# First FFN's up projection: transposing gated tiles into the other factor's buffer, and one adding transfer of each quad as an add on VectorE

## The chip, the cores and the metric

The kernel runs on one core of a Trainium2 chip. Its engines work side by side, each through its own instructions in order: TensorE (PE in the profile; PEld is its loading of weights), VectorE (DVE), ScalarE (ACT), GpSimd (POOL) and SyncE (SP, which here only issues transfers). Sixteen DMA engines carry the transfers; those of SyncE go out on the hardware queue q1, those of GpSimd on the software queue q0. The metric is the device time of one execution in microseconds.

## The reference

One layer of a diffusion backbone on 256 context and 256 latent tokens of width 2048: a half-step FFN, a mixer (attention heads beside bidirectional mLSTM heads), a second half-step FFN on the latent tokens, and a final norm, all with conditioned norms. The change touches only the first half-step FFN, which runs on all 512 tokens:

```python
def half_step_ffn(x, mod, i, g, w_up, w_down):
    h = adaln(x, g, mod, i)
    a, b = jnp.split(h @ w_up, 2, axis=-1)
    return x + 0.5 * mod[:, i + 2, None, :] * ((jax.nn.silu(a) * b) @ w_down)
```

The width of the hidden layer is 5632, that is 11 blocks of 512 columns. `mod` comes from the conditions through a weight matrix of its own (`w_mt` here), all of it in float32.

## The kernel before

**Products.** Every float32 product is made as three products of a rounded part and a rest (`hi` and `lo`): `hi*hi`, `hi*lo`, `lo*hi` (`mm3`, L152). So each weight tile of 128 x 2048 is split before use, in two halves of 1024 columns: ScalarE writes `hi` (L128), VectorE subtracts and writes `lo` (L129). There are four buffers of each, two tiles' worth. Where a helper records operations, the profile gives the helper's line for all of its callers.

**Up projection, block 0** is made beside the opening of the kernel. **Blocks 1 to 10** are made one after the other by `quad(n)`. It is a scheme of seven products instead of eight on halves of the token block and of the depth: the left factors are the token forms `a11, a12, n1, s4, s2, s3, a22` (fixed, made once, held in SBUF), the right ones are sums of weight parts, and the results add up in PSUM banks `X`, `Y`, `Z`. The list `order` has the seven with their sources; each is done for `q` = 0 and 1, one weight tile each, so that a quad has 14 steps, numbered 0 to 13 here (step 2m + q), of 24 products each.

**Where the weight sums come from.** `part(n, ab, c)` is a stored tile of 1 MB: ab = 0 for the gate's weights A, 1 for the other factor's B. Two tiles `chain_[q]` stay for the stage. At steps 0 and 1 they hold an A part. As soon as a step has split its tile, GpSimd issues an adding transfer (`accum`, L740) that adds the next part into it: a B part for `n1` (steps 4 and 5), another B part for `s2` (steps 8 and 9), another A part for `a22` (steps 12 and 13); then `again` loads the next quad's first part. Steps 2 and 3 use tiles loaded plain (`plain`, L910). Steps 6 and 7 use `ra[q]`, loaded by `loaded` (L905), the same B part that was added to `chain_[q]` after step 4 or 5; then a further part is added into `ra[q]`, which serves steps 10 and 11. That makes eight adding transfers in a quad. The tiles of `plain` and `loaded` are the four users of three buffers (`raw_tile`), in turn.

**The way out of PSUM.** At the end of a product, `use` copies or adds banks on ScalarE and VectorE: `p1` and `c11` make one gate tile in `ca` (silu on ScalarE, L868 and L890), `kept` copies a bank to `cy`, `p35` one to `c12`; `c12`, `c22` and `c21` add the second bank and multiply gate and other factor into `ca` (L851, L852). `ca`, `cy` and `c12` have two buffers each. A finished `ca` tile is put on the list `turn`. At the next step with q = 0, after half of its products, `turned` takes one from it: VectorE transposes it in blocks into the one buffer `stg` (L842) and SyncE stores `stg` to the hidden tensor in HBM (L844). The tiles of a quad are so stored at its steps 10 and 12 and at steps 0 and 2 of the next.

**Beside it** run the products of the modulation (`mod_items`): 96 weight tiles of 512 KB through two `sraw` buffers, issued by SyncE (L237), each multiplied and summed by VectorE (L208) with condition vectors of the context and the latent tokens in `cBh`. The vectors cover half of the depth; at half way both are loaded anew (L203), and the code holds the products back three steps (`WAIT = 3`).

**Down projection.** It begins with `pair(0)`: VectorE makes sums of hidden tiles by `first_plan`, and results go to `acc` (first copies L1078, adds L1080), in memory that the up stage's tiles had.

**The order of the work.** Each engine's order is fixed when the kernel is built, by a planner that takes instructions as their inputs and buffers come free by its costs, and otherwise as the code has them; instructions given to `keep_in_program_order` (`pinned`) keep their order among each other. Waits for data and for buffers are then added.

Of the kernel before, what the change touches and what calls it, by code (L numbers as in the profile page):

```python
# [9 lines left out]
F32 = mybir.dt.float32  # L10
# [9 lines left out]
P = 128  # L20
# [15 lines left out]
N_HID = 3  # L36

N_TURN = 2

PACE = (4, 2), (12, 13), (19, 19), (27, 28), (35, 37), (42, 44), (51, 51), (58, 54), (65, 61), (70, 70), (73, 76), (74, 85), (79, 96)  # L40
PACE += (86, 102), (92, 109), (98, 118), (100, 130), (103, 144), (106, 152), (109, 163), (112, 170), (128, 181)
# [5 lines left out]
CB = 512  # L47
# [11 lines left out]
def tile_layer(ctx: ExitStack, tc: tile.TileContext, I: dict, out: bass.AP):  # L59
    nc = tc.nc  # L60
# [12 lines left out]
    def bank():  # L73
        return ps["mm"].tile([P, 512], F32, tag="mm", name="mm")
# [619 lines left out]
    hidd = [dr.tile([4, P, CB] if n else [P, 16, P], F32, name=f"hid{n}") for n in range(NF // FB)]  # L694
# [6 lines left out]
    def form(tag, name):  # L701
        sp = ft if tag == "t" else fm
        return [sp.tile([P, 2, 8, P], F32R, tag=f"{tag}{x}", name=f"{name}{x}") for x in "hl"]
# [9 lines left out]
    def pinned(ins):  # L713
        tc.keep_in_program_order(ins)
# [22 lines left out]
    chp = chcm.__enter__()  # L737

    chain_ = [chp.tile([P, 2048], F32, name=f"chain{c}") for c in range(2)]
    accum = lambda dst, src: nc.gpsimd.dma_start(dst, src, accum_op=ALU.add)  # L740
    with pool(name="f1u", bufs=1) as f1u:
# [7 lines left out]
        def ca_tile():  # L749
            return f1u.tile([P, CB], F32, tag="ca", name="ca", bufs=2)  # L750
# [9 lines left out]
        def part(n, ab, c):  # L760
            return I["w_up1b"][n - 1, ab, c]

        def first_chain(n, c):
            nc.sync.dma_start(chain_[c], part(n, 0, c))
# [16 lines left out]
        n1, s2, s4 = form("n", "n1"), form("s", "s2"), form("t", "s4")  # L781
# [3 lines left out]
        a11, a12, a21, a22 = quarter(0, 0), quarter(0, 1), quarter(1, 0), quarter(1, 1)  # L785
# [43 lines left out]
        forms = token_forms()  # L829
        steps(forms, 2)  # L830
        turn = []
        last_turn = []

        def turned():

            if not turn:
                return
            n, t, ca = turn.pop(0)

            def staged():  # L840
                stg = chp.tile([P, CB], F32, tag="stg", name="stg")
                pinned(nc.vector.transpose(stg, ca))  # L842
                s, tt = divmod(t, 2)
                nc.sync.dma_start(hidd[n][2 * tt + s], stg)  # L844

            if (n, t) == (NB - 1, 3):
                last_turn.append(staged)
            else:
                staged()

        add = lambda o, x, y: nc.vector.tensor_tensor(o, x, y, op=ALU.add)  # L851
        negative = lambda o, y: nc.vector.scalar_tensor_tensor(o, o, -1.0, y, op0=ALU.mult, op1=ALU.mult)  # L852

        def c12_tile():
            return f1u.tile([P, CB], F32, tag="c12", name="c12", bufs=2)

        def quad(n, after=lambda step: None):

            X, Y, Z = {}, {}, {}
            ca, cy, cb, ra = {}, {}, {}, {}  # L860

            def p1(s):
                ca[s] = ca_tile()
                nc.scalar.activation(ca[s], X[s], AF.Copy)

            def c11(s):
                add(ca[s], Z[s], ca[s])
                nc.scalar.activation(ca[s], ca[s], AF.Silu)  # L868

            def kept(s):  # L870
                cy[s] = f1u.tile([P, CB], F32, tag="cy", name="cy", bufs=2)
                nc.scalar.activation(cy[s], Y[s], AF.Copy)

            def p35(s):
                cb[s] = c12_tile()
                nc.scalar.activation(cb[s], Y[s], AF.Copy)

            def c12(s):
                add(cb[s], X[s], cb[s])
                negative(ca[s], cb[s])  # L880
                turn.append((n, 2 * s, ca[s]))

            def c22(s):
                add(cy[s], X[s], cy[s])
                ca[s] = ca_tile()
                nc.scalar.activation(ca[s], X[s], AF.Copy)

            def c21(s):
                add(ca[s], Y[s], ca[s])
                nc.scalar.activation(ca[s], ca[s], AF.Silu)  # L890
                negative(ca[s], cy[s])
                turn.append((n, 2 * s + 1, ca[s]))

            def chained(ab, c):
                return lambda q: accum(chain_[q], part(n, ab, c + q))

            def again(q):
                if n + 1 < NB:
                    first_chain(n + 1, q)
                else:  # L900
                    nc.sync.dma_start(chain_[q], I["w_dn1"][0, 2 * q])

            def loaded(q):
                ra[q] = raw_tile()
                nc.sync.dma_start(ra[q], part(n, 1, 2 + q))  # L905
                return ra[q]

            def plain(q):
                r = raw_tile()
                nc.sync.dma_start(r, part(n, 0, 2 + q))  # L910
                return r

            held = lambda q: chain_[q]
            order = (
                (a11, held, X, True, chained(1, 0), p1),
                (a12, plain, Z, True, None, c11),
                (n1, held, Y, True, chained(1, 2), kept),
                (s4, loaded, Y, False, lambda q: accum(ra[q], part(n, 1, q)), p35),
                (s2, held, X, False, chained(0, 2), c12),
                (s3, lambda q: ra[q], X, False, None, c22),  # L920
                (a22, held, Y, True, again, c21),
            )
            for m, (a, src, dst, fresh, then, use) in enumerate(order):
                if fresh:
                    dst.update({s: bank() for s in range(2)})
                for q in range(2):
                    wt = split(src(q))
                    if then:
                        then(q)
                    after(2 * m + q)  # L930
                    for s in range(2):
                        for j in range(4):
                            k = 4 * q + j
                            hi, lo = a[0][:, s, k, :], a[1][:, s, k, :]
                            mm3(dst[s], hi, lo, *wt(slice(j * CB, (j + 1) * CB)), fresh and k == 0, k == 7, True)
                        if q and use:
                            use(s)
                        elif not s:
                            turned()
# [123 lines left out]
    def pair(p):  # L1063

        X, Y, Z, ra = {}, {}, {}, {}
# [8 lines left out]
        w = lambda m, cb: I["w_dn1"][2 * p + m, cb]  # L1074
# [41 lines left out]
        def loaded(m, cb):  # L1116
            raw = raw_tile()
            nc.sync.dma_start(raw, w(m, cb))
            return raw
# [9 lines left out]
        held = lambda c: chain_[c]  # L1129
# [14 lines left out]
        for m, (g, src, dst, fresh, then, use) in enumerate(order):  # L1144
            a = place0[m] if p == 0 and m < 2 else place[g]
            for c in range(2):
                wt = split(src(c))
                if then:
                    then(c)
                added()  # L1150
                if p == 0 and 2 * m + c == 1:
                    last_turn.pop()()
                for x in todo.get(2 * m + c, "").split():
                    if x.startswith("raw"):
                        hid_load(2 * p + 2 + int(x[3]), raws[int(x[3])])
                    else:
                        make[x]()
                if p == NP - 1:
                    if (2 * m + c) in GATES:
                        ahead.append(both_gates(GATES[2 * m + c]))  # L1160
                    if 2 * m + c == 13:
                        last_gate(0)
                        last_gate(1)
                    if m in (1, 4, 6):
                        gates = used[c] = ahead.pop(0)
                    elif m == 5:
                        gates = used[c]
                for s in range(2):
                    if fresh:
                        dst[c, s] = tbank() if c and dst is not X else bank()  # L1170
                    for j in range(FB):
                        k = slice((2 * j + s) * P, (2 * j + s + 1) * P)
                        mm3(dst[c, s], a[:, 0, k], a[:, 1, k], *wt(slice(j * CB, (j + 1) * CB)), fresh and j == 0, j == FB - 1, True)
                    use(c, s)
# [92 lines left out]
    with ExitStack() as mx:  # L1267
# [626 lines left out]
        for cb in range(NCB):  # L1894
# [8 lines left out]
            c = slice(cb * CB, (cb + 1) * CB)  # L1903
# [36 lines left out]
    with f2x:  # L1940
# [66 lines left out]
        a11, a12, a21, a22 = quarter(0, 0), quarter(0, 1), quarter(1, 0), quarter(1, 1)  # L2007
        forms2 = {g: f3.tile([P, 2, 8, P], F32R, tag=f"f{i}", name=f"{g}f") for i, g in enumerate(("n1", "s4", "s2", "s3"))}
        n1, s4, s2, s3 = ([x[:, 0], x[:, 1]] for x in (forms2[g] for g in ("n1", "s4", "s2", "s3")))
# [39 lines left out]
        turn = []  # L2049
        summed = set()  # L2050
        born, clock = {}, [0]

        def turned():
# [3 lines left out]
            n, t, sa, sign = turn[0]  # L2057
            if clock[0] < born[n, t] + N_TURN:
                return
# [383 lines left out]
```

## Time and profile before

| | us |
|---|---|
| runs | 2604.68, 2603.30, 2600.16 |
| median | 2603.3 |
| the profiled execution, its time | 2598.59 |
| its span | 2596.9 |
| TensorE busy | 2559.5 |
| VectorE busy | 2205.3 |
| ScalarE busy | 1404.3 |
| quads 1 to 10 | about 156 to 934 |
| mean granted TensorE clock | 0.993 of full |

Lines of the profile read so: start, duration, engine, line, operation, out<-in, shapes, count; in brackets the idle time of the engine just before it and what ended it. A group's line has total and mean duration, then the idle time before its members. The DMA lines give count, size and the median time from issue to landing. Matmuls overlap in the pipeline: each is shown with 0.39 us, and they start 0.227 us apart when nothing stops them.

### The profile page before, as it was taken

The page shows a single profiled execution, that of the slowest core. Times are in us where ns is not written, and L with a number is a line of the kernel's source. Part 1 is how long each engine was busy: PE and PEld are TensorE (multiplying, and loading weights), DVE is VectorE, ACT ScalarE, POOL GpSimd, SP SyncE. Part 2 cuts the span into 40 slices and gives each one's busy share as a digit, 9 for nine tenths or more (in the row PEclk, how much of TensorE's full clock was granted, in tenths as well). Part 3 has the DMA queues.
Part 4 walks back from the last instruction along what each step waited for, and adds up shares of the span by engine and source line. Part 5 has one row for each costly group of instructions (what it writes and reads, how often), then busy time and mean ns, then how long its engine had stood idle before and what let it go on. Part 6 is the DMA issues. An engine that isn't in the chain of part 4 may idle for free. (4 is left out here: it accounts for less than half of the span.)

```text
span 2596.9 us, 33840 instructions
## 1 busy us (share of the span) xinstructions
PE 2559.5 (99%) x12486; PEld 2126.6 (82%) x12486; DVE 2205.3 (85%) x2924; ACT 1404.3 (54%) x1798; POOL 222.0 (9%) x271
## 2 busy tenths in 40 slices
PE   8999999999999999999999999999999999999998
PEld 5788888878887878888889989888898888888886
DVE  7789888878888788888887899798889888888987
ACT  4454444444444455444454448456476676666763
POOL 0000000100000100000110000120000000000001
PEclk8999999999999999999999999999999999999999
DMA  9889999999999989999986897776768999999985
GB/s 395 348 217 276 267 284 277 263 269 279 264 290 269 263 239 243 212 221 233 225 256 256 292 328 241 241 277 218 266 230 248 275 272 279 285 282 279 272 250 167
DMA packets 153477, 684.69 MB, mean 264 GB/s; under 512 B 22872, under 2 KB 43864, under 8 KB 92000
## 3 DMA queue, kind: packets, MB, share of 16 engines
q1 hardware_dynamic: 123936, 490.64, 51.5%
q0 software_dynamic: 29376, 191.90, 37.2%
q8 instruction: 98, 1.61, 0.2%
q14 instruction: 67, 0.55, 0.1%
HBM read 664.59 MB, written 17.89 MB: 263 GB/s over the span
## 5 line engine op out<-in xcount | busy, mean ns | idle before, releaser
L128 ACT ACTIVATE hi<-raw 128x1024 fp32r<-128x1024 f32 (+2 forms) x488 | 504.3, 1040 | 401.7 <-PE mm L152 304.1
L129 DVE TENSOR_TENSOR lo<-raw,hi 128x1024 fp32r<-128x1024 f32 (+2 forms) x476 | 566.4, 1202 | 109.6 <-ACT hi L128 91.4
L128 ACT ACTIVATE hi<-chain 128x1024 fp32r<-128x1024 f32 x352 | 369.9, 1059 | 351.6 <-PE mm L152 200.4
L129 DVE TENSOR_TENSOR lo<-chain,hi 128x1024 fp32r<-128x1024 f32 x352 | 424.4, 1218 | 88.8 <-ACT hi L128 78.9
L152 PE MATMUL mm<-lo,hhi 128*128 128x512 f32 (+3 forms) x1024 | 388.3, 379 | 6.4 <-DVE lo L129 6.3
L152 PE MATMUL mm<-hi,hhi 128*128 128x512 f32 (+3 forms) x1024 | 390.9, 382 | 0.0
L152 PE MATMUL mm<-hi,hlo 128*128 128x512 f32 (+3 forms) x1024 | 387.1, 378 | 0.0
L208 DVE SCALAR_TENSOR_TENSOR junk<-sraw,cBh 128x1024 fp8e5<-128x1024 f32 x192 | 234.1, 1219 | 38.1 <-DMA sraw<-in_w_mt 36.3
L152 PEld LDWEIGHTS mm<-lo,hhi 128*128 128x128 f32 x1024 | 193.1, 189 | 42.2 <-DVE lo L129 8.7
L152 PEld LDWEIGHTS mm<-hi,hlo 128*128 128x128 f32 x1024 | 193.3, 189 | 32.2
L152 PEld LDWEIGHTS mm<-hi,hhi 128*128 128x128 f32 x1024 | 193.3, 189 | 31.8
L129 DVE TENSOR_TENSOR lo<-ra,hi 128x1024 fp32r<-128x1024 f32 x104 | 126.0, 1221 | 25.7 <-ACT hi L128 22.0
L128 ACT ACTIVATE hi<-ra 128x1024 fp32r<-128x1024 f32 x104 | 110.0, 1061 | 65.7 <-PE mm L152 39.7
L152 PE MATMUL mm<-lo,hid2h 128*128 128x512 f32 x352 | 137.1, 390 | 0.1
L152 PE MATMUL mm<-hi,hid2h 128*128 128x512 f32 x352 | 137.0, 389 | 0.0
L152 PE MATMUL mm<-hi,hid2l 128*128 128x512 f32 x352 | 137.0, 389 | 0.0
L152 PE MATMUL mm<-hi,sumshl 128*128 128x512 f32 x400 | 123.2, 389 | 0.0
L740 POOL DMA_DIRECT2D chain<-in_w_up1b x60 | 53.1, 886 | 734.2 <-DVE lo L129 573.8
L208 DVE SCALAR_TENSOR_TENSOR sr<-sr,cBl 128x1024 f32<-128x1024 f32 x84 | 102.1, 1223 | 14.0 <-DMA sr<-in_w_mt 13.1
L152 PE MATMUL mm<-hi,sumshh 128*128 128x512 f32 x352 | 108.9, 391 | 1.3 <-DVE acc L1080 1.3
L152 PE MATMUL mm<-hhi,hi 128*128 128x512 f32 (+1 forms) x288 | 101.4, 352 | 0.0
L152 PE MATMUL mm<-hhi,lo 128*128 128x512 f32 (+1 forms) x288 | 99.0, 344 | 0.0
(488 smaller groups left out, 5416.2 us busy)
## 6 DMA issues: line engine op xcount, KB each, us to landing
raw<-in_w_dn SPq DMA_DIRECT2D x70, 1024.0 KB, 9.8
chain<-in_w_up1b POOLq DMA_DIRECT2D x60, 1024.0 KB, 10.7
sraw<-in_w_mt SPq DMA_DIRECT2D x96, 512.0 KB, 8.5
sr<-in_w_mt SPq DMA_DIRECT2D x81, 512.0 KB, 5.5
raw<-in_w_up1b SPq DMA_DIRECT2D x40, 1024.0 KB, 9.1
mraw<-in_w_m SPq DMA_DIRECT2D x32, 1024.0 KB, 7.5
chain<-in_w_dn POOLq DMA_DIRECT2D x30, 1024.0 KB, 10.0
chain<-in_w_up2b POOLq DMA_DIRECT2D x28, 1024.0 KB, 10.5
```

The source lines that it names most:

```text
L128: scalar[0].activation(hi, src, AF.Copy)
L129: vector[0].tensor_tensor(lo, src, hi.bitcast(F32), op=ALU.subtract)
L152: tensor[0].matmul(out_ap, s, m, start=first and not n, stop=last and n == 2, skip_group_check=skip)
L208: ins = nc.vector.scalar_tensor_tensor(junk() if junk else raw, raw, 1.0, cB[s], op0=ALU.mult, op1=ALU.mult, accum_out=mT[:, i, s, kt, h : ...
L740: accum = lambda dst, src: nc.gpsimd.dma_start(dst, src, accum_op=ALU.add)
```

## The change

Two parts. First, each entry of `turn` carries along the tile of the other factor (`cb[s]`, of the pool's tag `c12`, or `cy[s]`), and the transpose writes into that tile instead of `stg`. Only the very last tile of the stage, whose store may outlast the pool, still goes to `stg`; it is transposed with the others at the end of the up stage, where before it was put off to step 1 of `pair(0)`.

Second, in quads 2 to 10, for q = 0 alone, the B part that was added to `chain_[0]` by a transfer after step 4 is added by VectorE from `ra[0]`, which holds the same part: half of it in step 5, the other half in step 6. `ra[0]` is for that asked for in step 3 instead of step 6. The transfer that then adds a further part into `ra[0]` comes behind the second add. For q = 1 everything stays.

```diff
+SUMMED = (0,)
...
-            n, t, ca = turn.pop(0)
-
-            def staged():
-                stg = chp.tile([P, CB], F32, tag="stg", name="stg")
-                pinned(nc.vector.transpose(stg, ca))
-                s, tt = divmod(t, 2)
-                nc.sync.dma_start(hidd[n][2 * tt + s], stg)
-
+            n, t, ca, spare = turn.pop(0)
             if (n, t) == (NB - 1, 3):
-                last_turn.append(staged)
-            else:
-                staged()
+                spare = chp.tile([P, CB], F32, tag="stg", name="stg")
+            pinned(nc.vector.transpose(spare, ca))
+            s, tt = divmod(t, 2)
+            nc.sync.dma_start(hidd[n][2 * tt + s], spare)
...
-                turn.append((n, 2 * s, ca[s]))
+                turn.append((n, 2 * s, ca[s], cb[s]))
...
-                turn.append((n, 2 * s + 1, ca[s]))
+                turn.append((n, 2 * s + 1, ca[s], cy[s]))
...
+            own = SUMMED if n > 1 else ()
+
+            def summed(q, h):
+                w = slice(h * 1024, (h + 1) * 1024)
+                add(chain_[q][:, w], chain_[q][:, w], ra[q][:, w])
+
+            def second(q):
+                if q not in own:
+                    chained(1, 2)(q)
+                if q - 1 in own:
+                    summed(q - 1, 0)
+
+            def third(q):
+                if q in own:
+                    if q == 1:
+                        summed(q, 0)
+                    summed(q, 1)
+                accum(ra[q], part(n, 1, q))
+
             held = lambda q: chain_[q]
             order = (
                 (a11, held, X, True, chained(1, 0), p1),
-                (a12, plain, Z, True, None, c11),
-                (n1, held, Y, True, chained(1, 2), kept),
-                (s4, loaded, Y, False, lambda q: accum(ra[q], part(n, 1, q)), p35),
+                (a12, plain, Z, True, lambda q: q - 1 in own and loaded(q - 1), c11),
+                (n1, held, Y, True, second, kept),
+                (s4, lambda q: ra[q] if q in own else loaded(q), Y, False, third, p35),
...
-                if p == 0 and 2 * m + c == 1:
-                    last_turn.pop()()
```

More of the change, by code (lines that the diff above doesn't have):

```diff
@@ L831, in tile_layer @@
         turn = []
-        last_turn = []
         def turned():
```

## The prediction

> **What bounds the kernel now.** I read the page's busy times first, then what TensorE waited for in the stage that the change touches, then that stage cut into its quads, and last the lines around the stalls.
>
> ```profile
> PE 2559.5 (99%) x12486; PEld 2126.6 (82%) x12486; DVE 2205.3 (85%) x2924; ACT 1404.3 (54%) x1798; POOL 222.0 (9%) x271
> ```
>
> ```profile
> PE mm L152 <- DVE lo L129: 9.1, 5, 3.5
> ```
>
> The second line is the whole list of TensorE's waits from 140 to 930 us: five, all for a `lo` half that VectorE had not yet written. Now the same stage, one window for each quad, from its first product with `n1` (step 4 of 14) to the next quad's:
>
> ```profile
> core 0: us, PE busy (x) PEld busy (x) DVE busy (x) ACT busy (x) POOL busy (x), PEclk, DMA share, GB/s
> 177.55:253.71 76.16, 76.16 (x338) 63.06 (x336) 62.00 (x77) 36.05 (x41) 7.07 (x8) 1.00 0.98 263
> ...
> 406.05:483.86 77.81, 76.94 (x337) 62.84 (x336) 68.36 (x90) 35.32 (x40) 7.09 (x8) 1.00 0.97 273
> 483.86:567.42 83.56, 79.54 (x337) 64.95 (x336) 64.36 (x83) 35.92 (x41) 7.95 (x9) 0.96 0.97 272
> 567.42:643.58 76.16, 76.16 (x338) 63.08 (x336) 65.53 (x84) 35.59 (x40) 6.26 (x8) 1.00 0.98 269
> 643.58:719.99 76.41, 76.41 (x339) 63.11 (x338) 67.58 (x94) 35.66 (x40) 6.98 (x8) 1.00 0.98 271
> ...
> 796.19:877.32 81.13, 78.19 (x338) 63.97 (x336) 70.31 (x92) 37.19 (x42) 7.94 (x9) 0.98 0.99 278
> ```
>
> Every window holds the same matmuls, about 337. An unstalled one takes 76.16 us with TensorE busy throughout, so the stage cannot go below that. Above it lie 1.65 (77.81), 7.40 (83.56), 0.25 (76.41) and 4.97 us (81.13): 14.3 us in all. That is what the change can win in these quads. VectorE works 62 to 70 us of each window and the DMA engines are busy 0.97 to 0.99 of it, so both are nearly full behind TensorE.
>
> **The transposes, the large stall.** Queries of VectorE, SyncE and TensorE around 545 us, with the landing of the store issued at 545.02:
>
> ```profile
> 557.65 0.71 DVE L842 STREAM_TRANSPOSE stg<-ca 128x512 f32<-128x512 f32 x1 [8.69 <-DMA hid<-stg]
> 558.29 2.31 DVE L129 TENSOR_TENSOR lo<-raw,hi 128x1024 fp32r<-128x1024 f32 x2
> ...
> 540.32 0.33 SPq L203 DMA_DIRECT2D cBh<-ccd  x1
> ...
> 542.44 0.49 SPq L203 DMA_DIRECT2D cBh<-ccd  x1
> 545.02 0.33 SPq L844 DMA_DIRECT2D hid<-stg  x1
> ...
> 559.52 0.80 PE L152 MATMUL mm<-lo,hhi 128*128 128x512 f32 x1 [3.54 <-DVE lo L129]
> ...
> DMA to landing us min/median/max: 12.5/12.5/12.5
> ```
>
> There is one `stg`. The second transpose of a pair may not overwrite it before the first one's store has landed. Here that store stands behind two 512 KB loads of the condition vectors and takes 12.5 us; VectorE, which works in order, waits 8.69 us with the next `lo` halves queued behind the transpose, and TensorE runs dry. The idle 3.54 us is followed by a granted clock of 0.96 over the window; idle and slow clock together are the 7.40 us.
>
> After the change each transpose writes the tile of its own other factor (`c12` or `cy`, two each), which VectorE itself has just finished reading. The wait has no cause left: **-7.40 us**. What is late next there? The `hi` halves for these products were done at once after (the `lo` needed no wait at 558.29), and the store may now take its time until its tile is taken again. For `cy` that is step 5 of the next quad, for `c12` step 7. The second `cy` transpose belongs to step 2, so three steps are left, 3 x 76.16/14 = 16.3 us, against a longest landing of 12.5 us. Behind a `cy` tile not yet free would stand ScalarE's copy `kept` of a PSUM bank, and behind that the products of step 6, which add into the same bank. The cover is thin by 3.8 us at the worst landing seen, ample at the median. I cost it at nothing.
>
> The transposes themselves stay, 702 ns each, and no DMA is added or dropped by this part. The very last one, of quad 10, moves from step 1 of the first down pair to the end of the stage, ahead of that pair's sums of hidden tiles on VectorE. Before:
>
> ```profile
> 938.94 0.70 DVE L842 STREAM_TRANSPOSE stg<-ca 128x512 f32<-128x512 f32 x1
> ...
> 943.72 0.71 DVE L842 STREAM_TRANSPOSE stg<-ca 128x512 f32<-128x512 f32 x1 [1.83 <-DMA hid<-stg]
> ...
> 944.52 1.58 ACT L1078 ACTIVATE acc<-mm 128x512 f32<-128x512 f32 x3 [4.32 <-issue]
> ...
> DMA to landing us min/median/max: 2.3/6.4/12.5
> ```
>
> (The last line is that of all 40 stores.) It no longer waits 1.83 us. But the first copies into `acc` start right when the last reader of the up stage's tiles ends (944.43), as their memory is the same; now a store reads from that memory too. Issued at about 939.7, it lands at 946.1 by the median, 1.7 us later than 944.43. So between -1.8 and, with 12.5 us, +7.8 us; I take **0**, the middle of no wait and a median store.
>
> **The add moved to VectorE.** Rows of the groups and of the DMA queues over 253 to 878 us, and of the same kind of add as the second FFN has it:
>
> ```profile
> L208 DVE SCALAR_TENSOR_TENSOR junk<-sraw,cBh 128x1024 fp8e5<-128x1024 f32 x169 | 206.1, 1219 | 37.9 <-DMA sraw<-in_w_mt 36.3
> ...
> L842 DVE STREAM_TRANSPOSE stg<-ca 128x512 f32<-128x512 f32 x32 | 22.5, 702 | 14.2 <-DMA hid<-stg 14.2
> ...
> q0 software_dynamic: 9238, 67.29, 54.6%
> ...
> chain<-in_w_up1b POOLq DMA_DIRECT2D x48, 1024.0 KB, 10.7
> ...
> raw<-in_w_up1b POOLq DMA_DIRECT2D x16, 1024.0 KB, 13.3
> ...
> L2089 DVE TENSOR_TENSOR chain<-chain,ra x20: 1212/1216/1226, 1978.6 to 2484.2; 128x1024 f32<-128x1024 f32 x20
> ```
>
> *Removed*: nine transfers, one in each of quads 2 to 10, each 0.88 us of issue on GpSimd, which is nearly idle. The 48 + 16 adding transfers hold all engines for 0.546 x 624 us / 64 = 5.3 us each. The factor was loaded twice (once added, once as `ra`), so this traffic goes away altogether. *Added*: 18 adds of 1.216 us on VectorE, 2.43 us a quad, and no load: `ra[0]` is asked for three steps earlier in the code, but the third staging buffer decides when it goes out. *Waits*: the first add of a quad needs `ra[0]`, and the transfer into `ra[0]` now waits for the second one. `ra[0]` is an old load by then: in the quad of 308 us its transfer went out at 290.78, some 45 us before step 5.
>
> ```profile
> 290.78 0.33 SPq L905 DMA_DIRECT2D raw<-in_w_up1b  x1
> ```
>
> Behind the adds on VectorE stand the `lo` halves of steps 6 and 7. Where these have no room the adds stall TensorE:
>
> ```profile
> 338.23 2.35 DVE L129 TENSOR_TENSOR lo<-raw,hi 128x1024 fp32r<-128x1024 f32 x2
> ...
> 344.42 2.35 DVE L129 TENSOR_TENSOR lo<-raw,hi 128x1024 fp32r<-128x1024 f32 x2
> ...
> 341.23 0.39 PE L152 MATMUL mm<-lo,s4h 128*128 128x512 f32 x1
> ...
> 346.67 0.39 PE L152 MATMUL mm<-lo,s4h 128*128 128x512 f32 x1
> ...
> 415.37 4.63 DVE L129 TENSOR_TENSOR lo<-raw,hi 128x1024 fp32r<-128x1024 f32 x4
> ...
> 417.41 0.39 PE L152 MATMUL mm<-lo,s4h 128*128 128x512 f32 x1
> ```
>
> In the quad of 308 us the first half for step 6 was ready at 339.4 and used at 341.23 (room 1.8), for step 7 at 345.6 and used at 346.67 (room 1.1): the one add ahead of step 6 fits, the two ahead of step 7 are 2.43 - 1.1 = 1.3 too long. In the quad of 384 us step 6 has 0.9 of room (416.5 to 417.41): 0.3 too long. In the others I take VectorE's present waits, 36.3 us for the `sraw` loads and 14.2 us for `stg`, as the room: together more than the 21.9 us of adds. **+1.7 us**, rounded up from 1.6; the bounds are nothing and all 18 adds, 21.9 us.
>
> **The relief of the DMA.** The other stall, in the window of 81.13:
>
> ```profile
> 810.21 2.35 DVE L129 TENSOR_TENSOR lo<-raw,hi 128x1024 fp32r<-128x1024 f32 x2
> 818.10 1.23 DVE L208 SCALAR_TENSOR_TENSOR junk<-sraw,cBh 128x1024 fp8e5<-128x1024 f32 x1 [5.54 <-DMA sraw<-in_w_mt]
> ...
> 805.64 0.33 SPq L237 DMA_DIRECT2D sraw<-in_w_mt  x1
> ...
> DMA to landing us min/median/max: 12.4/12.4/12.4
> ...
> 798.40 0.88 POOL L740 DMA_DIRECT2D chain<-in_w_up1b  x1 [15.64 <-DVE lo L129]
> ...
> 808.29 0.88 POOL L740 DMA_DIRECT2D raw<-in_w_up1b  x1 [3.79 <-DVE lo L129]
> ...
> 821.80 0.80 PE L152 MATMUL mm<-lo,s2h 128*128 128x512 f32 x1 [2.82 <-DVE lo L129]
> ```
>
> VectorE waits 5.54 us for a modulation load that took 12.4 us while adding transfers were in flight. The one issued at 798.40 is the one that goes. By its median landing of 10.7 it was in flight until 809.1, 3.5 us of the load's time. TensorE stood only 2.82 us, so a load 3.5 us shorter would have spared it all; but the adds put the load's issue up to 1.2 us later. Between 0 and -4.97 us; I take half, **-2.5 us**.
>
> Against this stands the Trainium skill, "DMA: Bandwidth & Descriptors", section "Queues, rings and completion order": each DMA engine alternates between the queues that have work, a packet at a time. By it the load's share does not depend on how many adding transfers are queued, only on whether one is. This trace has others in flight beside the load in any case, which agrees, and no run here yet shows the load without one; by it this term is 0.
>
> **The sum.** -7.4 + 0 + 1.7 - 2.5 = -8.2 us on the profiled execution's 2598.59: 2590.4. That execution is 4.7 us below the median of the runs shown (2603.3), so on that scale 2595.1. The quads' smaller excesses I leave as they are.
>
> **Rivals.**
> (1) *All stalls of these quads go*, since VectorE's waits for DMA shrink everywhere: -14.3, 2589.0. For it: each stall ends on a `lo` that VectorE brought late after such a wait. Against: VectorE gets 2.43 us more in the same quads.
> (2) *VectorE becomes the bound at steps 5 to 7* and shows its adds to TensorE: 18 x 1.216 - 7.4 = +14.5, 2617.8. For it: rooms of 1.1 and 0.9 us. Against: the unstalled windows with VectorE busy at 62 to 68 of 76 us. It decides from (7.4 + 5.2)/1.216 = 10 shown adds on, with 5.2 us (0.2%) as about what a measurement here can tell from no change.
> (3) *The stall at 545 us keeps its length with another owner*: the condition vectors issued at 542.44 are awaited by the next modulation product, which also stands in VectorE's queue. If it is ordered ahead of the `lo` halves VectorE waits nearly as long; 7.4 stays, 2.5 goes and 1.7 comes: -0.8, 2602.5. Against: the code holds these products back three steps after that load.
> (4) *The modulation loads gain nothing*, as other adding transfers are in flight beside them: -7.4 + 1.7 = -5.7, 2597.6. For it: another, issued at 808.29, ran beside the load of 12.4 us. By the page's rule just named, this is the case to expect.
>
> **How the numbers follow.** Forecast 0.38, (1) 0.20, (2) 0.13, (3) 0.14, (4) 0.15. The range runs from 2585 (rival 1, and the end of the stage at its best) to 2606 (rival 2 with half its adds shown: 10.9 - 7.4 = +3.5, 2606.8). Faster by over 0.2%: 0.36 of the forecast's, all of (1), 0.09 of (4), 0.65 in all; slower: (2) and 0.02 for a late store at the stage's end, 0.15; the rest, 0.20, is within.
>
> **What would show it.** Right: no wait of a transpose for a store, the window around 545 us at 76.2, the row of adds at 18 x 1.22, adding transfers from `w_up1b` 71 instead of 80, and the window around 820 us between 76 and 79. Wrong: TensorE waiting for `lo` at steps 6 and 7 in several quads (rival 2), ScalarE's copy into `cy` waiting for a store, or a new wait for `sraw` or the condition vectors where the large stall was.

## The result and the profile after

| | before | after |
|---|---|---|
| median, 8 runs each, same comparison | 2601.53 us | 2593.14 us |
| lowest and highest | 2596.10, 2604.68 | 2590.05, 2594.61 |
| ratio, 95% interval | | 0.9968 (0.9959 to 0.9978) |
| the profiled execution | 2598.59 | 2593.71 |

The kernel became 8.4 us faster, by the medians. The forecast was 8.2 us. (In a later comparison its ratio was 0.9981, 0.9972 to 0.9989, that is 5.1 us by the medians; the two intervals overlap.) The total is right, but two of its four terms were much too small, and they have opposite signs.

The busy times of the changed kernel come first, then all that TensorE waited for from 130 to 930 us:

```profile
PE 2557.9 (99%) x12486; PEld 2123.5 (82%) x12486; DVE 2223.8 (86%) x2942; ACT 1403.2 (54%) x1798; POOL 213.8 (8%) x262
```

```profile
PE mm L154 <- DVE lo L131: 3.9, 5, 2.4
```

VectorE has its 18 instructions more (2942 against 2924) and GpSimd its nine fewer. TensorE's waits fell from 9.1 to 3.9 us, and all are still for a `lo` half. The same windows as before, from the first product with `n1` of one quad to the next quad's (start:end, length, busy time of each engine, granted clock, DMA share, GB/s; the last row is all nine quads together):

```profile
core 0: us, PE busy (x) PEld busy (x) DVE busy (x) ACT busy (x) POOL busy (x), PEclk, DMA share, GB/s
...
405.47:481.73 76.26, 76.26 (x338) 62.99 (x336) 67.47 (x89) 35.71 (x40) 6.18 (x7) 1.00 0.93 261
481.73:559.25 77.52, 77.18 (x337) 62.68 (x336) 67.68 (x85) 35.94 (x41) 6.20 (x7) 1.00 0.92 267
...
635.41:712.99 77.58, 77.03 (x340) 62.94 (x338) 70.46 (x97) 35.48 (x40) 6.17 (x7) 1.00 0.91 256
...
789.19:867.24 78.05, 77.44 (x337) 62.67 (x336) 71.97 (x93) 35.60 (x41) 6.16 (x7) 1.00 0.91 263
...
176.99:867.24 690.25, 688.75 (x3027) 566.52 (x3026) 612.49 (x790) 321.87 (x361) 55.63 (x63) 1.00 0.93 264
```

The same row for the kernel before:

```profile
177.55:877.32 699.77, 691.95 (x3028) 570.11 (x3026) 596.48 (x775) 321.95 (x361) 63.57 (x72) 0.99 0.98 273
```

Nine unstalled windows of 76.16 us make 685.44, so the stalls of these quads fell from 14.3 to 4.8 us, 9.5 us less. Where the transposes made the large stall (VectorE and SyncE of the changed kernel round 545 us; start, duration, engine, line, operation, tiles):

```profile
542.75 0.70 DVE L842 STREAM_TRANSPOSE cy<-ca 128x512 f32<-128x512 f32 x1
...
545.08 2.35 DVE L131 TENSOR_TENSOR lo<-raw,hi 128x1024 fp32r<-128x1024 f32 x2
547.35 0.70 DVE L842 STREAM_TRANSPOSE cy<-ca 128x512 f32<-128x512 f32 x1
548.13 2.54 DVE L131 TENSOR_TENSOR lo<-raw,hi 128x1024 fp32r<-128x1024 f32 x2
...
540.90 0.49 SPq L205 DMA_DIRECT2D cBh<-ccd  x1
543.48 0.33 SPq L844 DMA_DIRECT2D hid<-cy  x1
```

The store again stands behind the loads of the condition vectors, and it and the one behind it land late, after 12.4 and 10.9 us. But the second transpose starts at 547.35 and waits for nothing. All that VectorE waited for from 177 to 935 us (total, times, longest):

```profile
DVE lo L131 <- ACT hi L130: 66.8, 36, 4.9
DVE junk L210 <- DMA sraw<-in_w_mt: 20.2, 13, 3.1
DVE ca L847 <- ACT ca L885: 1.6, 3, 0.7
DVE c L846 <- PE mm L154: 0.6, 1, 0.6
```

No transpose and no product waits for a store or for condition vectors. What is left in the stage is small and late. In the last quad (ScalarE, VectorE, TensorE):

```profile
908.33 1.06 ACT L722 ACTIVATE hidh<-hidh 128x1024 fp32r<-128x1024 f32 x1 [7.41 <-DMA hidh<-hid]
...
910.37 1.23 DVE L131 TENSOR_TENSOR lo<-chain,hi 128x1024 fp32r<-128x1024 f32 x1 [4.94 <-ACT hi L130]
...
915.67 0.50 PE L154 MATMUL mm<-lo,hhi 128*128 128x512 f32 x1 [2.36 <-DVE lo L131]
```

ScalarE waits 7.41 us for a hidden tile that is read back. The `hi` behind it is late, so the `lo` is late, and TensorE stands 2.36 us.

Over the same nine quads VectorE's products of the modulation, its adds, and the transfers read so: count, total and mean of one, then the idle time before them; of a queue, its packets, MB and share of the 16 engines; of transfers, their size and the median time to landing.

```profile
L210 DVE SCALAR_TENSOR_TENSOR junk<-sraw,cBh 128x1024 fp8e5<-128x1024 f32 x183 | 223.3, 1220 | 21.6 <-DMA sraw<-in_w_mt 20.2
...
L846 DVE TENSOR_TENSOR chain<-chain,raw 128x1024 f32<-128x1024 f32 x18 | 21.8, 1221 | 0.1
```

```profile
q0 software_dynamic: 9216, 67.11, 50.0%
...
raw<-in_w_up1b POOLq DMA_DIRECT2D x18, 1024.0 KB, 11.9
```

Before, these products waited 36.3 us for `sraw`, in the same quads:

```profile
L208 DVE SCALAR_TENSOR_TENSOR junk<-sraw,cBh 128x1024 fp8e5<-128x1024 f32 x184 | 224.3, 1219 | 38.0 <-DMA sraw<-in_w_mt 36.3
```

The order of the instructions on each engine behind the first FFN is the same in both kernels. The two profiled executions end 4.9 us apart, though the first FFN is done 9.3 us earlier (VectorE's last add into `acc` ends at 1362.7 against 1372.0 us): about 3 us of that went in the mixer and about 1.5 in the second FFN, with the same orders. I take that as the difference between two executions of the same work, which was not tried separately; the ratio over all runs stands for the result.

### The profile page after: what moved, and what is told of

It is laid out like the page before. It is cut to its first block, busy times and chain, and to the rows that moved or that the text cites. A ratio compares the mean times of both kernels' runs of the same rounds, so it can differ in the third digit from the quotient of the medians.

```text
span 2592.0 us, 33866 instructions
## 1 busy us (share of the span) xinstructions
PE 2557.9 (99%) x12486; PEld 2123.5 (82%) x12486; DVE 2223.8 (86%) x2942; ACT 1403.2 (54%) x1798; POOL 213.8 (8%) x262
## 5 line engine op out<-in xcount | busy, mean ns | idle before, releaser
L210 DVE SCALAR_TENSOR_TENSOR junk<-sraw,cBh 128x1024 fp8e5<-128x1024 f32 x192 | 234.2, 1220 | 21.6 <-DMA sraw<-in_w_mt 20.2
L210 DVE SCALAR_TENSOR_TENSOR sr<-sr,cBl 128x1024 f32<-128x1024 f32 x84 | 102.2, 1224 | 13.5 <-DMA sr<-in_w_mt 6.8
L742 POOL DMA_DIRECT2D chain<-in_w_up1b x51 | 45.1, 885 | 734.4 <-DVE lo L131 586.7
## 6 DMA issues: line engine op xcount, KB each, us to landing
chain<-in_w_up1b POOLq DMA_DIRECT2D x51, 1024.0 KB, 10.5
```

What stands on the lines that cost most here:

```text
L210: ins = nc.vector.scalar_tensor_tensor(junk() if junk else raw, raw, 1.0, cB[s], op0=ALU.mult, op1=ALU.mult, accum_out=mT[:, i, s, kt, h : ...
```

## The experiments

My theory at this point: the transposes bring their 7.4 us, the adds cost little, the transfers taken away bring a little. The rivals: the adds cost much more and the relief pays for them; the stall keeps its length under another owner; the relief is nothing. Each kernel below is timed against the kernel before in the same comparison. "Nine quads" is the length of the nine windows together in its profiled execution (before 699.77, after 690.25, unstalled 685.44). It is one execution: a second one of the changed kernel had 692.70, and two of a kernel further down 690.21 and 686.91. So a difference of up to some 3 us between two kernels in this number alone shows nothing.

### The transposes alone

```diff
-SUMMED = (0,)
+SUMMED = ()
```

> The changed kernel with the first part alone: every transpose goes into the other factor's tile, and all eight adding transfers of each quad stay. Theory (the two parts are separate, and the transposes carry nearly all): the window around 545 us falls from 83.56 to about 76.2, the window around 820 us stays near 81, and the time is 7.4 us below before, within 1 us of the changed kernel. Rival A (the lighter DMA load carries the gain): less than 4 us below before, with the waits of VectorE for sraw near 36 us as before and the stall at 545 us partly back. Rival B (the transposes' waits had also caused the other stalls): the window around 820 us falls to 77 without any relief, and the time is 10 us or more below before.

Measured: 2594.12 us, ratio 0.9975 (0.9964 to 0.9987), so 6.4 us less than before. Nine quads: 694.63. Two windows and the products of the modulation:

```profile
329.20:407.31 78.11, 76.47 (x338) 63.02 (x336) 66.17 (x87) 35.82 (x40) 6.16 (x7) 1.00 0.98 273
...
485.24:562.44 77.20, 76.70 (x337) 62.88 (x336) 65.56 (x84) 35.90 (x41) 7.93 (x9) 1.00 0.98 282
```

```profile
L210 DVE SCALAR_TENSOR_TENSOR junk<-sraw,cBh 128x1024 fp8e5<-128x1024 f32 x184 | 224.7, 1221 | 47.3 <-DMA sraw<-in_w_mt 45.8
```

The window of 83.56 us is down to 77.20: 6.4 us gone there. But a window that had no stall before is now 78.11 long, another that had 76.41 is 78.15, and the waits for `sraw` rose from 36.3 to 45.8 us. The window round 820 us, expected to stay near 81, fell to 78.34 with all transfers kept. The DMA share stays 0.98. So a part of the gain comes back as later waits for loads. That the long stall had been a rest in which the transfers caught up would explain it; it is argued, not shown.

### The adds alone

The function `turned()`, the `turn.append` lines and the late `last_turn` of the kernel before are put back; the rest of the changed kernel stays.

> The kernel before with the second part alone: one staging tile and the late last transpose as before, and VectorE adds for q = 0 in quads 2 to 10. Theory: the stall around 545 us stays (window 83 us), the adds cost 1.7 us and the relief brings 2.5, so 0 to 2 us below before. Rival A: 4 us or more below before, since the store behind the condition vectors lands earlier too. Rival 2 of the prediction (VectorE as the bound): slower than before by 3 us or more, with new waits for lo at steps 6 and 7.

Measured: 2598.85 us, ratio 0.9997 (0.9986 to 1.0009): no difference from before. Nine quads: 696.88. The window of the large stall, and the transposes:

```profile
483.07:565.45 82.38, 78.56 (x338) 63.77 (x336) 66.45 (x84) 35.68 (x41) 6.19 (x7) 0.98 0.90 259
```

```profile
L844 DVE STREAM_TRANSPOSE stg<-ca 128x512 f32<-128x512 f32 x36 | 25.3, 704 | 15.1 <-DMA hid<-stg 15.1
```

With one `stg` the stall is there again (82.38), and the transposes wait 15.1 us for it. The second part of the change moves nothing by itself. Either both of its terms are small, or they are large and cancel; the next two runs separate them.

### The transfer taken away, without the add

```diff
-add(chain_[q][:, w], chain_[q][:, w], ra[q][:, w])
+pass
```

> The changed kernel without the adds on VectorE: the transfers stay away and nothing is added in their place, so the B part is missing from the sum for q = 0. It has the relief of the DMA and not its price. Theory: 1.7 us below the changed kernel (the adds' price), quads at 76.2 to 77. Rival (the adds are hidden wholly): within 0.5 us of the changed kernel. Rival 2 of the prediction: 5 us or more below the changed kernel.

Measured: 2585.50 us, ratio 0.9943 (0.9930 to 0.9957). Nine quads: 686.77, only 1.3 us above the floor.

```profile
L210 DVE SCALAR_TENSOR_TENSOR junk<-sraw,cBh 128x1024 fp8e5<-128x1024 f32 x184 | 224.6, 1220 | 24.1 <-DMA sraw<-in_w_mt 22.5
```

Against the transposes alone, in the same comparison, nine adding transfers are gone and `ra[0]` is asked for earlier: 0.9943 - 0.9975 = -0.0032, 8.3 us. The waits for `sraw` fell from 45.8 to 22.5 us, and TensorE's waits from 130 to 930 us from 8.1 to 0.8 us. The relief is thus more than three times my term of 2.5 us and far from nothing. Against the changed kernel the difference is the 18 adds: 0.9968 - 0.9943 = 0.0025, 6.5 us; the 0.9968 is of another comparison, and with the later 0.9981 it would be 9.9 us.

### The adds, with the transfer kept

```diff
-add(chain_[q][:, w], chain_[q][:, w], ra[q][:, w])
+nc.vector.tensor_tensor(junk8, ra[q][:, w], ra[q][:, w], op=ALU.add, saturate=False)
...
-if q not in own:
-    chained(1, 2)(q)
+chained(1, 2)(q)
```

> The changed kernel with all eight adding transfers back, and its 18 adds on VectorE of the same size and place made into a scratch tile: the price without the relief. Theory: 1.7 us above the kernel with the first part alone, so about 5.7 us below before; sraw waits of VectorE about 36 us again. Rival (the relief does nothing, the adds are hidden): equal to the changed kernel. Rival (without the relief VectorE is the bound): 5 us or more above the kernel with the first part alone, with waits for lo in several quads.

Measured: 2598.91 us, ratio 0.9999 (0.9985 to 1.0012). Nine quads: 698.71. The nine quads' row:

```profile
177.18:875.89 698.71, 691.68 (x3027) 566.17 (x3026) 612.52 (x789) 321.13 (x361) 63.46 (x72) 1.00 0.98 273
```

Against the transposes alone the 18 adds, with `ra[0]` asked for earlier, cost 0.9999 - 0.9975 = 0.0024, 6.3 us, as above. VectorE's waits for `sraw` are 35.3 us here, 45.8 with the transposes alone: a part of the adds' time went where VectorE had waited. Against this kernel the changed one is 0.9968 - 0.9999 = -0.0031, 8.1 us better, again by the nine transfers; with the later 0.9981 it would be 4.7 us. So a second pair gives each size, but across two comparisons, and only as well as the changed kernel's ratio is known. Each such difference of two ratios is uncertain by 4 to 5 us (the root of the two half intervals' squares, 0.0017 to 0.0018 of 2600 us). Both sizes are clear of zero; the relief is clear of my 2.5 us within one comparison (8.3 +/- 4.6), the price of the adds lies only at the edge of it (6.3 +/- 4.6 against 1.7).

### The store that the transpose waited for

Of the kernel before, with the second load of the condition vectors left out:

```diff
-lambda h: conditions(halves, h, h + 1)
+lambda h: None if h else conditions(halves, h, h + 1)
```

> The kernel before without the second loading of the condition vectors (two loads of 512 KB at about 541 us): the later modulation products use the first half's vectors, all else as before. Theory (the store of 545 us is slow as it stands behind these loads): it lands in 6 to 9 us instead of 12.5, the transpose waits under 5 us, and the window around 545 us falls to 77 to 79. Rival (that store is slow for the adding transfers beside it): the landing stays at 11 to 13 us and the window at 82 to 84.

One execution: 2594.68 us beside a median of 2599.72 for the kernel before. The store, its landing and the transposes of that quad:

```profile
545.07 0.33 SPq L844 DMA_DIRECT2D hid<-stg  x1
...
DMA to landing us min/median/max: 4.5/4.5/4.5
```

```profile
L842 DVE STREAM_TRANSPOSE stg<-ca 128x512 f32<-128x512 f32 x2 | 1.4, 706 | 0.7 <-DMA hid<-stg 0.7
```

Without these two loads in front of it (a modulation load issued 3.0 us earlier stays) the same store lands in 4.5 us, not 12.5; the transposes wait 0.7 us, not 8.69; the window is 77.51 us. One buffer, and a store behind two loads, made the stall: that reading is shown. Of the 7.40 us about 6.1 go in this way; 77.51 and the changed kernel's 77.52 both stay 1.4 us above an unstalled window.

### The add on GpSimd

```diff
-add(chain_[q][:, w], chain_[q][:, w], ra[q][:, w])
+nc.gpsimd.tensor_tensor(chain_[q][:, w], chain_[q][:, w], ra[q][:, w], op=ALU.add)
```

The second FFN has a line with the same text, and the edit met that too; its adds went to GpSimd as well. The time of the run is therefore that of two stages, and only the windows speak for the first FFN.

> The changed kernel with its 18 adds made by GpSimd instead of VectorE. Theory after the first runs (the relief is worth about 8 us and the adds on VectorE cost about 6.5, as the kernel without the adds is at 0.9943 of before): GpSimd has the room, so the price goes and the time comes to 12 to 15 us below before, quads near 76.2 to 77. Rival A (adds on GpSimd are slow and stand in the way of its transfers): the add takes several us, adding transfers go out later, ScalarE waits longer for chain and raw, and the time is no better than the changed kernel. Rival B (GpSimd and VectorE block each other over SBUF): the lo subtractions, 1.22 us now, get longer, and TensorE waits for lo again.

Measured: 2652.42 us, ratio 1.0204 (1.0186 to 1.0222), slower. Nine quads: 711.63, 21.4 us above the changed kernel's.

```profile
L912 POOL TENSOR_TENSOR chain<-chain,raw 128x1024 f32<-128x1024 f32 x18 | 57.1, 3186 | 111.9 <-DVE lo L131 111.9
```

```profile
327.03 6.66 POOL L912 TENSOR_TENSOR chain<-chain,raw 128x1024 f32<-128x1024 f32 x2 [9.67 <-DVE lo L131]
...
331.95 2.81 DVE L210 SCALAR_TENSOR_TENSOR junk<-sraw,cBh 128x1024 fp8e5<-128x1024 f32 x1
```

The expectation fell by direction. An add takes 3.19 us on GpSimd, 2.6 times as long as on VectorE, and the next adding transfer stands behind it. It doesn't even leave VectorE free: a product of the modulation, 1.22 us otherwise, took 2.81 us while a pair of these adds ran, and its mean over the nine quads rose from 1220 to 1339 ns. This agrees with the Trainium skill, "SBUF — State Buffer", section "Who interferes with whom": a VectorE instruction with two inputs in SBUF contends with a GpSimd instruction that reads SBUF, as its second input comes through the shared read port.

### The add for q = 1 in place of q = 0, and for both

Here both halves of the add stand in step 7, behind the split of `ra[1]`, and `ra[1]` isn't asked for earlier than before.

```diff
-SUMMED = (0,)
+SUMMED = (1,)
...
-(s4, lambda q: ra[q] if q in own else loaded(q), Y, False, third, p35),
+(s4, lambda q: ra[q] if q in ra else loaded(q), Y, False, third, p35),
```

> The changed kernel with the add made for q = 1 instead of q = 0: same relief (one adding transfer less in a quad), same 18 adds, but both stand in step 7 behind the loading of ra[1], instead of steps 5 and 6. Theory (the price is VectorE's work, wherever it stands between steps 5 and 8): within 2 us of the changed kernel. Rival (the price comes from the tight steps 5 and 6): 3 to 6 us below the changed kernel, since VectorE has 3 to 5 us of room at steps 7 and 8.

Measured: 2583.55 us, ratio 0.9932 (0.9913 to 0.9952). It beats the kernel before and, across two comparisons, the changed kernel. My theory there, that it would be within 2 us of the changed kernel, fell; so I ran it again beside the changed kernel:

> The same kernel as the one with the add made for q = 1, beside the changed kernel on the same chip: 0.991 to 0.995 of before and 5 us or more below the changed kernel, if the gain is real; within 2 us of it, if the first timing was an accident.

> The changed kernel itself, as the measure for the others in this comparison: 0.996 to 0.998 of before by both theories.

Measured in the one comparison: 2586.88 us, ratio 0.9951 (0.9939 to 0.9963), against 2593.73 us, ratio 0.9981 (0.9972 to 0.9989), for the changed kernel: 6.9 us less. GpSimd's issues of adding transfers in the quad that begins round 760 us; first the changed kernel, then this one:

```profile
797.15 0.88 POOL L742 DMA_DIRECT2D chain<-in_w_up1b  x1 [21.36 <-DVE lo L131]
801.70 0.89 POOL L742 DMA_DIRECT2D raw<-in_w_up1b  x1 [3.68 <-DVE lo L131]
806.39 0.89 POOL L742 DMA_DIRECT2D raw<-in_w_up1b  x1 [3.79 <-DVE lo L131]
```

```profile
787.38 0.87 POOL L742 DMA_DIRECT2D chain<-in_w_up1b  x1 [14.83 <-DVE lo L131]
798.29 0.89 POOL L742 DMA_DIRECT2D raw<-in_w_up1b  x1 [10.04 <-DMA sraw<-in_w_mt]
803.99 0.88 POOL L742 DMA_DIRECT2D raw<-in_w_up1b  x1 [4.81 <-DVE lo L131]
```

With q = 0's transfer gone the three that remain here (behind steps 5, 6 and 7) go out within 9.2 us. With q = 1's gone the first comes a step earlier and the three spread over 16.6 us. It is so in each of the quads 2 to 9: counted from the quad's first product with `n1`, the first goes out at 5.2 to 8.0 us in the changed kernel and at -2.7 to 1.4 us here. Over the nine quads, landing and ScalarE's splits of `chain_` (again first the changed kernel, then this one):

```profile
L130 ACT ACTIVATE hi<-chain 128x1024 fp32r<-128x1024 f32 x145 | 151.4, 1057 | 152.9 <-PE mm L154 102.2 <-DMA chain<-in_w_up1b 45.3 <-issue 5.2
```

```profile
L130 ACT ACTIVATE hi<-chain 128x1024 fp32r<-128x1024 f32 x145 | 151.9, 1058 | 162.4 <-PE mm L154 135.3 <-DMA chain<-in_w_up1b 18.9 <-issue 5.2
...
L210 DVE SCALAR_TENSOR_TENSOR junk<-sraw,cBh 128x1024 fp8e5<-128x1024 f32 x184 | 224.5, 1220 | 12.1 <-DMA sraw<-in_w_mt 10.8
...
raw<-in_w_up1b POOLq DMA_DIRECT2D x18, 1024.0 KB, 8.9
```

The adding transfers into `ra` land in 8.9 us, not 11.9; ScalarE waits 18.9 us for `chain_`, not 45.3; VectorE waits 10.8 us for `sraw`, not 20.2. The other execution of each kernel differs in the same way (9.0 against 12.2, 20.4 against 54.6, 11.5 against 25.5).

A part of the gain that both pairs of executions show lies behind the nine quads. From the last quad's first product with `n1` to the first product with sums of hidden tiles the two executions of the changed kernel took 80.8 and 81.2 us, those of this kernel 76.2 both. The hidden tile for which ScalarE waited 7.41 us above (first the changed kernel, then this one) landed so:

```profile
DMA to landing us min/median/max: 29.8/29.8/29.8
```

```profile
DMA to landing us min/median/max: 13.5/13.5/13.5
```

It is 30.0 and 13.6 us in the other two executions. With 13.5 us ScalarE finds the tile ready, the `hi` behind it is not late, and TensorE's wait of 2.36 us is gone. Why it lands so much earlier wasn't tried. Two more runs take the halves of the change to q = 1 apart. The transfer of q = 1 taken away without an add (`pass` in `summed`, as above):

> The changed kernel with the adding transfer of q = 1 taken away instead of that of q = 0, and no add made in its place, so the B part is missing from the sum for q = 1: the relief alone, for the other transfer. Theory (one transfer is worth what the other is, 8 us over the first part alone): within 2 us of 0.9943 of before. Rival (taking away the later transfer of the two is worth more): 3 us or more below that.

Measured: 2581.40 us, ratio 0.9931 (0.9918 to 0.9944), nine quads 686.49. Without the adds q = 1 and q = 0 (0.9943, nine quads 686.77) can't be told apart in time. The rows of the transfers differ in the same way (for q = 0 ScalarE waits 34.4 us, and they land in 11.7 us):

```profile
L130 ACT ACTIVATE hi<-chain 128x1024 fp32r<-128x1024 f32 x145 | 152.0, 1058 | 162.9 <-PE mm L154 135.0 <-DMA chain<-in_w_up1b 16.4 <-issue 5.2
...
raw<-in_w_up1b POOLq DMA_DIRECT2D x18, 1024.0 KB, 9.9
```

And the adds at q = 1's places with all transfers kept (`dummy_add`'s edit of `summed` and `second` on this kernel):

> As the kernel with the 18 scratch adds at steps 5 and 6 (0.9999 of before), but with them behind the splitting of ra[1] at step 7; all eight adding transfers stay in both. Theory (the price of the adds is set by where they stand on VectorE): within 2.5 us of the kernel with the first part alone (0.9975), that is 4 us or more below the one with the adds at steps 5 and 6. Rival (the price is VectorE's work itself): equal to the one at steps 5 and 6, about 0 to 1 us below before.

Measured: 2595.40 us, ratio 0.9985 (0.9973 to 0.9997), nine quads 699.82 against 698.71 for q = 0. By time it is 0.0014 below q = 0's, with intervals that overlap: no difference is shown. (Its profiled execution, 2606.80 us, was the slowest of twelve, so its windows say little.)

The two halves, 0.0012 without the adds and 0.0014 with all transfers kept, are each within the noise, but together they would make up nearly all of the 0.0030 between the two kernels. So the runs can't say whether the place of the adds, the spacing of the transfers, or only both together bring the 6.9 us. At q = 1 the adds cost 0.9951 - 0.9931 = 0.0020, 5 +/- 4.6 us, which can't be told from the 6.3 us at q = 0. What makes q = 1 better stays open.

For both q the same edit has `SUMMED = (0, 1)`:

> The changed kernel with the adds for q = 0 and q = 1: two adding transfers less in each quad and 36 adds on VectorE. Theory (relief falls off as DMA is no longer full, price grows as VectorE fills up): VectorE at 70 to 74 us of a quad, slower than the changed kernel by 2 to 8 us. Rival (each pair has the same net worth of about -2 us): 2 us below the changed kernel.

Measured: 2588.29 us, ratio 0.9954 (0.9938 to 0.9970). Nine quads:

```profile
177.04:869.27 692.23, 689.32 (x3028) 566.66 (x3026) 628.28 (x805) 320.78 (x360) 48.49 (x55) 1.00 0.88 251
```

I had expected it slower than the changed kernel by 2 to 8 us; that isn't shown, as the intervals overlap (that kernel's is 0.9959 to 0.9978). The DMA share falls to 0.88 and VectorE's work rises to 628 of 692 us. That a second transfer taken away from each quad buys more than its adds cost isn't shown either.

## Why the prediction came out right, point by point

| term | predicted, us | measured, us | by |
|---|---|---|---|
| transposes, with the stage's end | -7.4 + 0 | -6.4 | transposes alone against before |
| adds on VectorE | +1.7 | +6.3 (second pair +6.5, or +9.9 by the later ratio) | adds with the transfer kept; without the adds |
| transfers taken away | -2.5 | -8.3 (second pair -8.1, or -4.7 by the later ratio) | without the adds, against transposes alone; the changed kernel against adds with the transfer kept |
| sum | -8.2 | -8.4 (later -5.1) | the changed kernel's medians |

**The transposes.** The mechanism was right at each step: the store landed late behind the two loads, the wait went with the buffer, and nothing new waits for the store of `cy` or `c12`: VectorE's list above has no store, and ScalarE's copies into `cy` waited for TensorE alone. The term was 1 us too large by time. In its place the stall window went to 77.2 to 77.5, not 76.2, and some waits for loads grew.

**The end of the stage.** The last quad from its `n1` products to the first down product, 54.4 us at the least, took 56.2 before and 57.7 after; what follows, up to the first product with sums of hidden tiles, took 24.2 before and 23.1 after. One gives back what the other gains, so 0, inside bounds of -1.8 and +7.8, is about what it is in the changed kernel. With the transposes alone the two together took 82.7 us, 2.3 more than before, and without the adds 77.3: this stretch depends on the other terms too, which the prediction didn't ask.

**The adds: the first step that failed.** I counted 1.6 us at three places of two quads. In the changed kernel these two quads' windows take 76.17 and 76.26 us, so nothing shows there. The price shows elsewhere: against the kernel without the adds in later windows (together 3.5 us, about what two executions can differ by) and behind the last quad's first product with `n1` (80.8 against 77.3 us). For the other quads I wrote: "In the others I take VectorE's present waits ... as the room: together more than the 21.9 us of adds." Those waits are room only in part: with the adds and all transfers kept they fell by 10.5 us, from 45.8 to 35.3. VectorE works in order and the adds stand in front of `lo` halves of steps 6 and 7; a wait for `sraw` at another step need not make room in front of these. Besides, the other half of the same edit shrinks those waits, from 45.8 to 22.5 us. About a third of the adds' 21.9 us shows.

**The relief: the second step that failed.** I took half of one stall, since I asked only whether the load of 12.4 us in one window would land in time. That stall didn't hang on the one transfer: the window of 81.13 us was down to 78.34 with the transposes alone, and 78.05 in the changed kernel, so the sign "between 76 and 79" came true without being evidence for the term. The adding transfers lay beside loads in every quad: 23 us of VectorE's waits for `sraw` went away in nine quads, and with them small stalls in many windows, also those that the transposes alone had left at 78.11 and 78.15 (76.16 and 77.09 without the transfers and the adds).

**The rivals.** (1) All stalls go: not with the adds; it is very nearly the kernel without them (nine quads 686.77). (2) VectorE becomes the bound: its mechanism was there, with 5 of the 18 adds' time (6.3/1.22), less than the 10 adds from which it was to decide. (3) Another owner of the stall: refuted, the window is 77.52 and no wait for condition vectors stands there. (4) The loads gain nothing: refuted by 8.3 us within one comparison. By the total alone it could not be told from the forecast, as the later 5.1 us lie near its 5.7. For this rival the prediction had a rule of the Trainium skill ("DMA: Bandwidth & Descriptors", section "Queues, rings and completion order"), that a DMA engine alternates between the queues with work. The runs don't refute the rule; they refute the step from it to a gain of 0. It says how two transfers in flight share an engine, and nothing of how much of the time one is in flight. That share of time fell with the nine transfers: the software queue held 55.2% of the engines' time with the transposes alone and 49.9% with the transfers gone, as its rows of these two kernels have it:

```profile
q0 software_dynamic: 10368, 75.50, 55.2%
```

```profile
q0 software_dynamic: 9216, 67.11, 49.9%
```

The total was right by luck: the two large misses, +4.6 and about -5.7 us, and the small one of +1.0 cancel. A right total was no evidence for its terms; the pairs of runs were needed.

## What to carry to other kernels

In an engine that works in order, look for the room of added work where that work stands: at what is queued directly behind it and when that is needed. The engine's waits in other places took up only a part of it here, 10.5 of 21.9 us. When traffic is removed from engines that are 0.98 busy, look for its worth in the sum of all waits for other loads, not in the one stall beside it. Where one of several equal transfers can go, try each: here q = 1's was 6.9 us better than q = 0's, and what fits, though it isn't shown, is that its absence spreads the others out in time.

## What the runs showed of the hardware that was not expected

- **A short wait can cost TensorE more than itself, and its length alone doesn't tell when.** Waits of 2.82 and 3.54 us came with a granted clock of 0.98 and 0.96 over their windows, which were 4.97 and 7.40 us too long. In the first run with the add for q = 1 one wait of 2.50 us, alone in its window, made it 4.4 us too long, at 0.98. But with the adds at q = 1's places and all transfers kept, a window with waits of 2.52 and 1.68 us kept 1.00 (second line):

```profile
329.30:409.87 80.57, 78.07 (x337) 64.12 (x336) 70.72 (x91) 35.92 (x40) 5.86 (x7) 0.98 0.90 257
...
330.89:411.88 80.99, 76.79 (x337) 62.92 (x336) 69.34 (x90) 35.59 (x40) 6.17 (x7) 1.00 0.94 259
```

- **A 256 KB store behind two 512 KB loads** on the same queue landed after 12.5 us; without them, in the one execution tried, after 4.5 us.
- **Spacing of adding transfers.** With the same number in each quad, but the first of them a step earlier, the 18 into `ra` landed in 8.9 us by the median and not 11.9.
- **GpSimd's add** of 128 x 1024 float32 values took 3.19 us and stretched a VectorE instruction from 1.22 to 2.81 us.
